# Sparse-attention layer on one core: compression MLP with high and low keys side by side, position term apart, x and key/value weights in one row

## The chip, the cores and the metric

One core of a Trainium2 chip runs the whole program. The metric is the device time of one execution in microseconds; the number compared is the median over runs. A core has the engines PE (TensorE: matmuls and their weight loads), DVE (VectorE), ACT (ScalarE), POOL (GpSimd) and SP (SyncE, which here issues nearly all DMAs). Each engine works through its instructions in order and waits for others by semaphores.

## The reference

One decoder layer of native sparse attention: 256 positions, width 2048, 16 query heads of 128 in 4 groups, one key and one value head per group and branch, all in float32. What matters here is the compressed branch; its keys and values come of a small MLP over blocks of 32 positions, one every 16:

```python
def nsa_compress(kv, pe, w1, w2):
    n_cmp = (kv.shape[1] - CMP_LEN) // CMP_STRIDE + 1          # 15 blocks
    idx = np.arange(n_cmp)[:, None] * CMP_STRIDE + np.arange(CMP_LEN)[None, :]
    blocks = kv[:, idx] + pe[None, None, :, None, :]
    hid = jax.nn.silu(jnp.einsum('bnlgd,lde->bnge', blocks, w1))
    return jnp.einsum('bnge,ef->bngf', hid, w2)

h = x @ w_in            # queries, three pairs of keys and values, gates, z
k_cmp, v_cmp = nsa_compress(kc, pe_k, w1_k, w2_k), nsa_compress(vc, pe_v, w1_v, w2_v)
...                     # compressed, selected and window attention, gated sum
y = (o * silu(z)) @ w_out
x = layer_norm(ALPHA * x + y)
```

## The kernel before

Every float32 operand is split into a rounded high part, written by ACT, and the remainder as low part, written by DVE (`split_into`, L72 to L74). A product is then three fast matmuls: high by high, high by low, low by high. For the projections x stands with high and low part side by side, so that one matmul of 512 columns (L110) does two of the three and one of 256 columns (L113) the third; `join` (L119) adds the halves.

*The key/value pass* (`kv_pass`, L161) comes first: 16 chunks of 128 rows of x and of the 1024 weight columns that give kc and vc, into 8 PSUM banks, 16 matmuls per chunk. x is loaded by `load_x` (L85) into tiles `kt` (4 buffers) and the weights into tiles `big` (8 buffers); chunk 0's weights come as three pieces, one of them on ACT's queue, the rest on SP's. From chunk 13 on the value half is held back (`LATE`) and done at the end. Six matmuls on zeros run ahead of it (`WARM`). The small tables are loaded at chunk 15 (`load_small`).

*Then* `kv_out` joins and splits kc into tiles with columns for 4 groups x 16 blocks and 2 for the position embedding (66 in all, `CM`), two projections of group 0 run (`proj_t`, 1 MB of weights each, loaded into `wraw`, 3 buffers, split in two halves into `whi` and `wlo`, 4 buffers each), `kv_out` does vc, and `compress_hidden` runs the first layer of the MLP for k, for v a little later: 16 rows, three matmuls of 256 columns each (L219 to L221), with the weights `w1` loaded as 1 MB twice and split into halves of 4 rows. PE's order up to the MLP for k is that of the source; the rest is ordered by a planner that gives each engine the ready instruction that comes first in the source. `compress_act` (L226) adds up the partial sums by two float32 matmuls against a 0/1 table `csel`, which also adds the position columns to each block; `compress_out` (L243) is the second layer.

*Then*, per group, `group_proj` (keys, four query heads, bias, a value projection), `attention` for the first 128 positions, `z_proj` (four gate projections) and `attention` for the rest; at the end the output projection, residual and normalization. `compress_act` and `compress_out` stand inside `group_proj(0)`, between key and query projections. Scores of the compressed branch read the columns 256 to 272 of the key tiles, which L323 copies.

## Time and profile before

| | us |
|---|---|
| median of 3 runs (487.21 to 487.33) | 487.32 |
| the profiled execution, its own time | 486.98 |
| its span, first to last instruction | 485.2 |
| PE busy (2822 matmuls) | 475.4 |
| DVE busy | 332.4 |
| ACT busy | 274.4 |
| DMA: 91.41 MB, share of 16 engines' time on SP's queue | 51.4% |

Read the table with care: a busy share is an average over stages, and PE's matmuls overlap, so that its busy time is longer than the sum of their steps. What a step costs on PE is read from the distance between the starts of two instructions in the timeline. The granted clock of PE was 0.997 over the execution.

### The profile page before, as it was taken

How to read it: one execution, taken by the hardware profiler on the slowest of the kernel's cores; microseconds unless marked ns; L12 is line 12 of the kernel's file. 1: busy time of each engine (PE TensorE's matmuls, PEld its weight loads, DVE VectorE, ACT ScalarE, POOL GpSimd, SP SyncE). 2: the span in 40 equal slices, each digit the busy share in tenths (PEclk: the TensorE clock that was granted, in tenths of full speed). 3: DMA queues.
4: the chain of work that ended last, by engine and by line, in shares of the span. 5: the costliest groups of instructions: out<-in, count | busy, mean ns of one | idle time of the engine just before them, and what ended most of it. 6: DMA issues, size and time to landing. Idle time of an engine off the chain costs nothing.

```text
span 485.2 us, 7570 instructions
## 1 busy us (share of the span) xinstructions
PE 475.4 (98%) x2822; PEld 416.8 (86%) x2823; DVE 332.4 (69%) x760; ACT 274.4 (57%) x543; POOL 9.6 (2%) x16
## 2 busy tenths in 40 slices
PE   7999999999999999999999999999999999999994
PEld 4888889899888889888889988888988888888893
DVE  4754887656878656777865686775577775597745
ACT  5653785447665645767555566654476644565411
POOL 1000000000000000000000000000000000000014
PEclk9999999999999999999999999999999999999998
DMA  7992579545443634363644534354436955357204
GB/s 271 404 365 112 174 257 331 202 175 175 173 175 130 225 131 174 99 247 104 224 162 174 173 151 133 153 182 173 151 111 223 377 199 192 140 174 261 86 1 173
DMA packets 18959, 91.41 MB, mean 188 GB/s; under 512 B 2404, under 2 KB 5591, under 8 KB 10219
## 3 DMA queue, kind: packets, MB, share of 16 engines
q1 hardware_dynamic: 18635, 90.54, 51.4%
q8 instruction: 22, 0.36, 0.3%
q10 hardware_dynamic: 288, 0.39, 0.2%
q14 instruction: 14, 0.11, 0.1%
HBM read 88.80 MB, written 2.12 MB: 187 GB/s over the span
## 4 chain that ended last, share of the span: by engine, by line
PE 96%; DMA 1%; DVE 1%; SPq 0%; ACT 0%; issue 0%; DVEq 0%
PE proj L110 33%; PE proj L113 17%; PE proj L509 3%; PE proj L508 3%; PE proj L507 3%; PE proj L337 3%; PE proj L336 3%; PE proj L335 3%; PE tr L430 2%; PE sc L509 2%; PE sc L507 2%; PE sc L508 2%; PE sc L110 1%; PE tr L110 1%; PE sc L383 1%; PE sc L385 1%
## 5 line engine op out<-in xcount | busy, mean ns | idle before, releaser
L110 PE MATMUL proj<-xs,whi 128*128 128x512 f32 x688 | 241.6, 397 | 2.2 <-ACT whi L73 1.8
L74 DVE TENSOR_TENSOR wlo<-wraw,whi 128x1024 fp32r<-128x1024 f32 (+1 forms) x134 | 164.0, 1228 | 89.9 <-ACT whi L73 89.5
L73 ACT ACTIVATE whi<-wraw 128x1024 fp32r<-128x1024 f32 (+1 forms) x134 | 142.1, 1063 | 114.8 <-PE proj L110 51.1
L113 PE MATMUL proj<-xs,wlo 128*128 128x256 f32 x688 | 188.0, 282 | 0.1
L110 PEld LDWEIGHTS proj<-xs,whi 128*128 128x128 f32 x688 | 127.9, 188 | 29.0 <-ACT whi L73 3.3
L113 PEld LDWEIGHTS proj<-xs,wlo 128*128 128x128 f32 x688 | 128.3, 188 | 3.2 <-DVE wlo L74 0.5
L393 ACT ACTIVATE t<-t,m 128x128 f32<-128x128 f32 (+3 forms) x96 | 37.6, 395 | 8.9 <-DVE m L391 8.8
L337 PE MATMUL proj<-wlo,xs 128*128 128x268 f32 x128 | 36.6, 286 | 0.0
L336 PE MATMUL proj<-whi,xs 128*128 128x268 f32 x128 | 36.6, 286 | 0.0
L335 PE MATMUL proj<-whi,xs 128*128 128x268 f32 x128 | 36.4, 285 | 0.0
L74 DVE TENSOR_TENSOR wlo<-big,whi 128x1024 fp32r<-128x1024 f32 (+2 forms) x18 | 19.8, 1106 | 13.7 <-ACT whi L73 11.8
L509 PE MATMUL proj<-whi,big 128*128 128x512 f32 (+1 forms) x76 | 28.6, 377 | 0.0
L508 PE MATMUL proj<-wlo,big 128*128 128x512 f32 (+1 forms) x76 | 28.6, 376 | 0.0
L507 PE MATMUL proj<-whi,big 128*128 128x512 f32 (+1 forms) x76 | 27.7, 376 | 0.0
L73 ACT ACTIVATE whi<-big 128x1024 fp32r<-128x1024 f32 (+2 forms) x18 | 17.3, 965 | 16.8 <-PE tr L110 9.1
L335 PEld LDWEIGHTS proj<-whi,xs 128*128 128x128 f32 x128 | 24.0, 188 | 0.4
L336 PEld LDWEIGHTS proj<-whi,xs 128*128 128x128 f32 x128 | 24.1, 188 | 0.1
L337 PEld LDWEIGHTS proj<-wlo,xs 128*128 128x128 f32 x128 | 24.1, 188 | 0.0
L122 DVE SCALAR_TENSOR_TENSOR join<-proj,join 128x256 f32<-128x256 f32 x43 | 17.9, 419 | 7.9 <-ACT join L121 7.9
L433 ACT ACTIVATE ph<-tr 128x512 fp32r<-128x512 f32 x24 | 14.1, 598 | 15.7 <-PE tr L430 15.6
L434 DVE TENSOR_TENSOR pl<-tr,ph 128x512 fp32r<-128x512 f32 x24 | 16.2, 687 | 5.9 <-ACT ph L433 5.5
L393 ACT ACTIVATION_READ_ACCUMULATOR t<-t,m 128x1 f32 x96 | 18.2, 190 | 0.0
(182 smaller groups left out, 662.2 us busy)
## 6 DMA issues: line engine op xcount, KB each, us to landing
wraw<-in_wt SPq DMA_DIRECT2D x40, 1024.0 KB, 4.9
wraw<-in_wo SPq DMA_DIRECT2D x16, 1024.0 KB, 5.0
wraw<-in_wv SPq DMA_DIRECT2D x8, 1072.0 KB, 5.5
...
wraw<-in_w_k SPq DMA_DIRECT2D x2, 1024.0 KB, 5.2
wraw<-in_w_v SPq DMA_DIRECT2D x2, 1024.0 KB
...
```

Of the source, the lines that this page charges most:

```text
L73: act.activation(hi, src, AF.Copy)
L74: pin(dve.tensor_tensor(lo, src, hi.bitcast(F32), op=ALU.subtract))
L110: pe.matmul(acc, hi, xk(k), start=(k == 0), stop=False)
L113: pe.matmul(acc[:, :SEQ], lo, xh(k), start=False, stop=(k == KC - 1))
L122: dve.scalar_tensor_tensor(t, acc[:, :SEQ], scale, t, op0=ALU.mult, op1=ALU.add)
L335: pe.matmul(a, xh(k)[:, ts], hi[:, k4, :], start=(k == 0), stop=False)
L336: pe.matmul(a, xl(k)[:, ts], hi[:, k4, :], start=False, stop=False)
L337: pe.matmul(a, xh(k)[:, ts], lo[:, k4, :], start=False, stop=(k == KC - 1))
L393: act.activation(tt, tt, AF.Exp, bias=m[:, i:i + 1], scale=-1.0, accum_out=den[:, i:i + 1])
L507: pin(pe.matmul(y, ah, hi[:, h2, c0:c1], start=(hq == 0 and h == 0), stop=False))
L508: pin(pe.matmul(y, ah, lo[:, h2, c0:c1], start=False, stop=False))
L509: pin(pe.matmul(y, al, hi[:, h2, c0:c1], start=False, stop=(hq == 3 and h == 3)))
```

## The change

x and the key/value weights are laid out as one array of 16 chunks, 128 rows of 1280 floats (5 KB): one load per chunk into the `wraw` tiles, chunk 0 in two pieces on SP's queue. x is split chunk by chunk (before: mostly by two), the weights of chunk 1 in two halves. Warm-up matmuls are 8 for 6. The small tables are loaded at chunk 8, in source order on SP's queue, with the one-hot table and 1 MB of w1 behind them. The key tiles hold high and low part side by side: the first layer is one matmul with all 128 weight columns against the high part of w1 and one with the 64 high ones against the low part. The position embedding leaves the key tiles; `add_pos` sums pe[l] * w1[l] over the 32 rows l on DVE into a 128x128 tile, for which w1 is loaded a second time in four pieces of 1 MB into the tile `t1` (1 buffer), and a third matmul in `compress_act` adds its column sums to each valid block. `compress_act` for k moves behind the query heads of group 0, that for v, `compress_out` and the copies of L323 behind the value projection. The host-side layout follows.

```diff
--- before.py
+++ after.py
@@ -32,11 +32,12 @@
 VW = 2 * P + 3 * HPG
 LU = 384
 KTW = 4 * P + 16
-CM = NG * 16 + 2
-FIRST = ((0, 256), (256, 512), (512, 1024))
-CUTS_X = (0, 1, 2, 4, 6, 8, 10, 12, 14, 16)
+CM = NG * 16
+FIRST = ((0, 512), (512, 1280))
+SPLITS = {0: ((0, 256), (256, 512), (512, 1024)), 1: ((0, 512), (512, 1024))}
 LATE = 13
-WARM = 6
+SMALL_AT = 8
+WARM = 8
 WARM_END = 8
 PARTS = ((0, 320), (320, 512))
 
@@ -82,16 +83,13 @@
 
     X2 = [None] * 4
 
-    def load_x(k0, k1):
-        raw = sb.tile([P, KTW], F32, name="kt", bufs=4)[:, :(k1 - k0) * SEQ]
-        raw = raw.rearrange("p (k s) -> p k s", s=SEQ)
-        nc.sync.dma_start(raw, A["xT"][k0 // 2][:, k0 % 2:k0 % 2 + k1 - k0, :])
-        c, o = divmod(k0, 4)
+    def split_x(k, raw):
+        c, o = divmod(k, 4)
         if o == 0:
             X2[c] = [xp.tile([P, 2, 2 * SEQ], F32R, name="xs") for _ in range(2)]
-        t = X2[c][o // 2][:, o % 2:o % 2 + k1 - k0, :]
-        hi, lo = t[:, :, :SEQ], t[:, :, SEQ:]
-        if k0 == 0:
+        t = X2[c][o // 2][:, o % 2, :]
+        hi, lo = t[:, :SEQ], t[:, SEQ:]
+        if k == 0:
             dve.tensor_copy(hi, raw)
             dve.tensor_tensor(lo, raw, hi.bitcast(F32), op=ALU.subtract)
         else:
@@ -137,9 +135,11 @@
         for n, shape in (("peT_k", [P, CLEN]), ("peT_v", [P, CLEN]), ("w2_k", [P, P]), ("w2_v", [P, P]),
                          ("rel", [2 * CSTRIDE, NH]), ("gmask", [P, 3 * HPG]), ("signs", [5, 2])):
             t = const.tile(shape, F32, name=n)
-            nc.sync.dma_start(t, A[n])
+            keep(nc.sync.dma_start(t, A[n]))
             small[n] = t
-        nc.sync.dma_start(csel, A["csel"])
+        keep(nc.sync.dma_start(csel, A["csel"]))
+        keep(nc.sync.dma_start(onehot, A["onehot"]))
+        keep(nc.sync.dma_start(first_w1, A["w1_k"][:, :8, :]))
 
     ident = const.tile([P, P], F32, name="ident")
     make_identity(nc, ident)
@@ -160,20 +160,14 @@
 
     def kv_pass():
         for k in range(KC):
-            if k in CUTS_X:
-                load_x(k, CUTS_X[CUTS_X.index(k) + 1])
-            raw = sb.tile([P, CSTRIDE * CM], F32, name="big", bufs=8)[:, :1024].rearrange("p (k n) -> p k n", k=1)
-            src = A["wkvc"][k][:, None, :]
-            if k == 0:
-                hi, lo = (wp.tile([P, 1, 1024], F32R, name=n, bufs=4) for n in ("whi", "wlo"))
-                for i, (n0, n1) in enumerate(FIRST):
-                    (act if i == 0 else nc.sync).dma_start(raw[:, :, n0:n1], src[:, :, n0:n1])
-                for n0, n1 in FIRST:
-                    split_into(hi[:, :, n0:n1], lo[:, :, n0:n1], raw[:, :, n0:n1], keep)
-            else:
-                nc.sync.dma_start(raw, src)
-                hi, lo = split_w(raw, 0, 1)
-            if k == KC - 1:
+            raw = wp.tile([P, SEQ + 1024], F32, name="wraw", bufs=3)
+            for n0, n1 in FIRST if k == 0 else ((0, SEQ + 1024),):
+                nc.sync.dma_start(raw[:, n0:n1], A["xw"][k, :, n0:n1])
+            split_x(k, raw[:, :SEQ])
+            hi, lo = (wp.tile([P, 1, 1024], F32R, name=n, bufs=4) for n in ("whi", "wlo"))
+            for n0, n1 in SPLITS.get(k, ((0, 1024),)):
+                split_into(hi[:, 0, n0:n1], lo[:, 0, n0:n1], raw[:, SEQ + n0:SEQ + n1], keep if k == 0 else lambda i: i)
+            if k == SMALL_AT:
                 load_small()
             kv_mms(k, hi, lo, 0, NG)
             if k < LATE:
@@ -184,16 +178,18 @@
             kv_mms(*args, NG, 2 * NG)
 
     def kv_out(which, name):
-        hi, lo = (sb.tile([P, CSTRIDE, CM], F32R, name="big", bufs=8) for _ in range(2))
+        kvc[name] = sb.tile([P, CSTRIDE, 2 * CM], F32R, name="big", bufs=4)
         for g in range(NG):
-            view = [t[:, :, g * 16:(g + 1) * 16].rearrange("p l n -> p n l") for t in (hi, lo)]
+            view = [kvc[name][:, :, c + g * 16:c + (g + 1) * 16].rearrange("p l n -> p n l") for c in (0, CM)]
             split_into(*view, join(accs[NG * which + g]).rearrange("p (n l) -> p n l", l=CSTRIDE))
-        view = [t[:, :, 64:66].rearrange("p l a -> p a l") for t in (hi, lo)]
-        split_into(*view, small["peT_" + name].rearrange("p (a l) -> p a l", a=2))
-        kvc[name] = hi, lo
-
-
-    csel = sb.tile([P, SEQ], F32, name="zth", bufs=1)[:CM].rearrange("p (a n) -> p a n", a=2)
+
+
+    onehot = sb.tile([P, 512], F32, name="ph", bufs=2)[:33, :LU]
+    first_w1 = sb.tile([P, 8, 2 * P], F32, name="t1", bufs=1)
+    csel = sb.tile([P, SEQ], F32, name="zth", bufs=1)[:, :2 * CM].rearrange("p (a n) -> p a n", a=2)
+    valid = const.tile([P, CM], F32, name="valid")
+    pool.memset(valid, 1.0)
+    pool.memset(valid.rearrange("p (g n) -> p g n", g=NG)[:, :, NCMP:], 0.0)
     kc_hi = const.tile([P, NG, 16], F32R, name="kc_hi")
     kc_lo = const.tile([P, NG, 16], F32R, name="kc_lo")
     vcs = const.tile([P, NG, P], F32R, name="vcs")
@@ -207,26 +203,48 @@
     phc = const.tile([P, HPG, P], F32R, name="phc")
     pool.memset(phc.bitcast(F32), 0.0)
 
+
+    pos = {n: const.tile([P, P], F32, name="pos_" + n) for n in "kv"}
+
+    def add_pos(name):
+        for l0 in (0, 8):
+            raw = first_w1 if (name, l0) == ("k", 0) else sb.tile([P, 8, 2 * P], F32, name="t1", bufs=1)
+            if raw is not first_w1:
+                nc.sync.dma_start(raw, A["w1_" + name][:, l0:l0 + 8, :])
+            for l in range(8):
+                for a in range(2):
+                    w, o = raw[:, l, a * P:(a + 1) * P], 16 * a + l0 + l
+                    pe_l = small["peT_" + name][:, o:o + 1]
+                    if o == 0:
+                        dve.tensor_scalar(pos[name], w, pe_l, None, op0=ALU.mult)
+                    else:
+                        dve.scalar_tensor_tensor(pos[name], w, pe_l, pos[name], op0=ALU.mult, op1=ALU.add)
+
+
     def compress_hidden(name):
-        part = bank("proj")[:CM, :2 * P]
-        hi, lo = kvc[name]
+        part = bank("proj")[:, :2 * P]
+        hl = kvc[name]
         for i in range(2):
             raw = load_w(A["w1_" + name][:, 8 * i:8 * i + 8, :], 8, 2 * P)
             for j in range(2):
                 wh, wl = split_w(raw, 4 * j, 4 * j + 4)
                 for l4 in range(4):
                     l = 8 * i + 4 * j + l4
-                    pe.matmul(part, hi[:, l, :], wh[:, l4, :], start=(l == 0), stop=False)
-                    pe.matmul(part, hi[:, l, :], wl[:, l4, :], start=False, stop=False)
-                    pe.matmul(part, lo[:, l, :], wh[:, l4, :], start=False, stop=(l == CSTRIDE - 1))
-        ps_sb = sb.tile([P, 512], F32, name="pl", bufs=2)[:CM, :2 * P]
+                    last = l == CSTRIDE - 1
+                    for lo in (True, False) if last else (False, True):
+                        if lo:
+                            pe.matmul(part[:CM], hl[:, l, :CM], wl[:, l4, :], start=False, stop=False)
+                        else:
+                            pe.matmul(part, hl[:, l, :], wh[:, l4, :], start=(l == 0), stop=last)
+        ps_sb = sb.tile([P, 512], F32, name="pl", bufs=2)[:, :2 * P]
         act.activation(ps_sb, part, AF.Copy)
         return ps_sb
 
     def compress_act(name, ps_sb):
-        acc = bank("sc")[:, :P]
+        acc = bank("sc")[:, :CM]
         for i in range(2):
-            pe.matmul(acc, ps_sb[:, i * P:(i + 1) * P], csel[:, i, :], start=(i == 0), stop=(i == 1))
+            pe.matmul(acc, ps_sb[:, i * P:(i + 1) * P], csel[:, i, :], start=(i == 0), stop=False)
+        pe.matmul(acc, pos[name], valid, start=False, stop=True)
         th = sb.tile([P, 512], F32, name="a", bufs=1)[:, :64]
         act.activation(th, acc[:, :64], AF.Tanh, scale=0.5)
         src = acc[:, :64].rearrange("p (g n) -> p g n", g=NG)
@@ -274,8 +292,6 @@
 
 
     rel_aug = const.tile([33, NH], F32, name="rel_aug")
-    onehot = sb.tile([P, 512], F32, name="ph", bufs=2)[:33, :LU]
-    nc.sync.dma_start(onehot, A["onehot"])
     dve.memset(rel_aug[32:33, :], MASKED)
     dve.tensor_scalar(rel_aug[0:32, :], small["rel"], -1.0, None, op0=ALU.mult)
     pu = bank("o")
@@ -306,7 +322,6 @@
             split_into(kt[0][:, o:o + P], kt[1][:, o:o + P], acc[:, half * P:(half + 1) * P])
         if g == 0:
             hv = compress_hidden("v")
-            compress_act("k", hk)
         split_into(kt[0][:, 272:528], kt[1][:, 272:528], join(early[1] if g == 0 else proj_t(10 * g + 1)))
         st["kt"] = kt
         st["q"] = []
@@ -315,12 +330,11 @@
             qt = [sb.tile([P, SEQ], F32R, name="q", bufs=10) for _ in range(2)]
             split_into(qt[0], qt[1], acc)
             st["q"].append(qt)
-            if g == 0 and h == 0:
-                compress_act("v", hv)
             if g == 0 and h == 1:
-                compress_out()
-        for t, s in zip(kt, (kc_hi, kc_lo)):
-            dve.tensor_copy(t[:, 256:272], s[:, g, :].bitcast(F32))
+                add_pos("k")
+        if g == 0:
+            compress_act("k", hk)
+            add_pos("v")
         st["bias"] = load_bias(g)
         accs = [bank("proj") for _ in range(2)]
         for h in range(2):
@@ -340,6 +354,11 @@
         for t in range(2):
             split_into(v[0][:, t, :], v[1][:, t, :], accs[t][:, :2 * P])
             act.activation(gt[:, t, :], accs[t][:, 2 * P:VW], AF.Tanh, scale=0.5)
+        if g == 0:
+            compress_act("v", hv)
+            compress_out()
+        for t, s in zip(kt, (kc_hi, kc_lo)):
+            dve.tensor_copy(t[:, 256:272], s[:, g, :].bitcast(F32))
         st["v"], st["gt"] = v, gt
         return st
 
@@ -441,8 +460,8 @@
 
     def gate(g, qt, o_ps):
         if qt == 0:
-            AH[g] = sb.tile([P, HPG, SEQ], F32R, name="big", bufs=8)
-            AL[g] = sb.tile([P, HPG, SEQ], F32R, name="big", bufs=8)
+            both = sb.tile([P, 2, HPG, SEQ], F32R, name="big", bufs=4)
+            AH[g], AL[g] = both[:, 0], both[:, 1]
         qs = slice(qt * P, (qt + 1) * P)
         a = sb.tile([P, HPG, P], F32, name="a", bufs=1)
         for h in range(HPG):
@@ -666,8 +685,7 @@
         return a.reshape(-1, P, a.shape[-1]).transpose(1, 0, 2)
 
     arr = {"x": x}
-    arr["xT"] = np.stack([rows(x.T[k:k + 2 * P]) for k in range(0, DM, 2 * P)])
-    arr["wkvc"] = w[:, 2048:3072].reshape(KC, P, 1024)
+    arr["xw"] = np.concatenate([x.T.reshape(KC, P, SEQ), w[:, 2048:3072].reshape(KC, P, 1024)], axis=2)
     wt = []
     for g in range(NG):
         cols = [3072 + g * P, 4096 + g * P]
@@ -699,11 +717,12 @@
     oh[:, :127] = 0.0
     oh[32, :127] = 1.0
     arr["onehot"] = oh
-    cs = np.zeros((CM, 2, P), np.float32)
+    cs = np.zeros((2, CM, 2, CM), np.float32)
     for g in range(NG):
         for n in range(NCMP):
             j = 16 * g + n
-            cs[j, 0, j] = cs[64, 0, j] = cs[j + 1, 1, j] = cs[65, 1, j] = 1.0
+            cs[:, j, 0, j] = cs[:, j + 1, 1, j] = 1.0
+    cs = cs.reshape(2 * CM, 2, CM)
     arr["csel"] = cs
     gm = np.ones((P, HPG, 3), np.float32)
     gm[:31, :, 0] = 0.0
```

## Rows read from the trace of the kernel before

**Rows 1.** page, engine table: busy us, share of the span, instructions

```profile
PE 475.4 (98%) x2822; PEld 416.8 (86%) x2823; DVE 332.4 (69%) x760; ACT 274.4 (57%) x543; POOL 9.6 (2%) x16
```

**Rows 2.** PE timeline, start: start us, length, line, tiles, count

```profile
1.19 2.74 PE L131 MATMUL tr<-zero 128*128 128x512 bf16 x6 [1.19 <-DVE zero L127]
...
4.31 1.19 PE L110 MATMUL proj<-xs,whi 128*128 128x512 f32 x3 [0.38 <-DVE xs L96]
...
9.49 0.96 PE L110 MATMUL proj<-xs,whi 128*128 128x512 f32 x3 [1.79 <-ACT whi L73]
...
12.73 0.85 PE L110 MATMUL proj<-xs,whi 128*128 128x512 f32 x3
...
15.55 0.86 PE L110 MATMUL proj<-xs,whi 128*128 128x512 f32 x3
...
51.92 0.40 PE L110 MATMUL proj<-xs,whi 128*128 128x512 f32 x1
```

**Rows 3.** windows: us, busy us and instructions by engine, clock, DMA share, GB/s

```profile
5.00:6.00 1.00, 1.00 (x8) 0.87 (x6) 0.00 (x0) 0.63 (x1) 0.00 (x0) 1.00 0.36 116
...
7.70:9.50 1.80, 0.01 (x2) 0.01 (x1) 0.33 (x2) 1.11 (x2) 0.00 (x0) 1.00 1.02 412
...
20.00:50.00 30.00, 30.00 (x172) 26.22 (x171) 15.43 (x19) 13.47 (x18) 0.00 (x0) 1.00 0.64 247
...
63.00:73.00 10.00, 10.00 (x80) 8.99 (x79) 9.17 (x15) 9.43 (x17) 0.00 (x0) 1.00 0.71 262
...
63.00:111.00 48.00, 48.00 (x337) 44.11 (x336) 33.09 (x51) 27.96 (x43) 0.53 (x1) 1.00 0.66 243
```

**Rows 4.** timeline of ACT, chunk 1's high-part split

```profile
8.38 1.06 ACT L73 ACTIVATE whi<-big 128x1024 fp32r<-128x1024 f32 x1 [0.84 <-DMA big<-in_wkvc]
```

**Rows 5.** DMA issues by line: count, KB each, median us to landing

```profile
wraw<-in_wt SPq DMA_DIRECT2D x40, 1024.0 KB, 4.9
```

**Rows 6.** timeline of SP's queue: the slowest of the small loads to issue

```profile
22.06 1.33 SPq L140 DMA_DIRECT2D gmask<-in_gmask  x1
```

**Rows 7.** timeline of PE, end of the pass and first MLP rows

```profile
50.05 0.40 PE L113 MATMUL sc<-xs,wlo 128*128 128x256 f32 x2
...
50.29 0.40 PE L113 MATMUL tr<-xs,wlo 128*128 128x256 f32 x2
...
63.15 0.28 PE L219 MATMUL proj<-whi,big 128*66 128x256 f32 x1
...
67.37 0.28 PE L219 MATMUL proj<-whi,big 128*66 128x256 f32 x1
```

**Rows 8.** chain of work that ended last: bias matmul, then combining k's sums

```profile
67.65 0.74 PE o L282 x2
...
72.87 0.45 PE sc L229 x4
```

**Rows 9.** timelines of DVE and PE, compression MLP

```profile
64.33 1.23 DVE L74 TENSOR_TENSOR wlo<-wraw,whi 128x1024 fp32r<-128x1024 f32 x1 [0.68 <-ACT whi L73]
...
71.62 1.23 DVE L74 TENSOR_TENSOR wlo<-wraw,whi 128x1024 fp32r<-128x1024 f32 x1
...
74.80 0.28 PE L220 MATMUL proj<-wlo,big 128*66 128x256 f32 x1
```

**Rows 10.** groups by shape: busy us, mean ns, idle before

```profile
L449 DVE SCALAR_TENSOR_TENSOR a<-o,zs 128x128 f32<-128x128 f32 x32 | 7.4, 283 | 1.1 <-PE o L439 0.6
```

**Rows 11.** timeline of DVE, dependent and independent small instructions

```profile
120.68 0.23 DVE L396 RECIPROCAL den<-den 128x12 f32<-128x12 f32 x1
...
120.94 0.17 DVE L399 TENSOR_TENSOR coef<-coef,den 128x12 f32<-128x12 f32 x1
...
141.37 0.69 DVE L449 SCALAR_TENSOR_TENSOR a<-o,zs 128x128 f32<-128x128 f32 x3
```

**Rows 12.** timelines of DVE and PE, first V projection tile of group 0

```profile
92.72 1.28 DVE L74 TENSOR_TENSOR wlo<-wraw,whi 128x1072 fp32r<-128x1072 f32 x1
...
100.09 0.29 PE L337 MATMUL proj<-wlo,xs 128*128 128x268 f32 x1
```

## The prediction

> **What bounds the kernel now.** I read the table of engines first: TensorE (PE) is busy 475.4 us, 98% of the span of 485.2 [rows 1]. A busy PE is not yet a PE without waits, so I read next where it waited. The order of its instructions at the start shows all of it: after six warm-up matmuls the first real one starts at 4.31 us, chunk 0 is done at about 7.7, chunk 1 starts at 9.49, chunk 2 at 12.73, chunk 3 at 15.55 (a full-speed chunk is thus 2.82 us), and the first projection after the key/value pass at 51.92 [rows 2]. Sixteen chunks at 2.82 us from 4.31 would end at 49.4, so 2.5 us are lost, nearly all in 7.70 to 9.50, where PE did nothing [rows 3]. From 12.7 us to about 475 us PE has no gap, so there each PE microsecond removed is worth a microsecond, but only while VectorE and ScalarE (ACT), which split every weight tile into a high and a low part ahead of PE, keep ahead of it. The windows by stage say where they hardly do: in 63 to 73 us (the compression MLP) VectorE (DVE) is busy 9.17 of 10 us [rows 3].
>
> The sum is made against the profiled execution: 486.98 us, that is 485.2 of span and 1.8 around it. The median of the runs shown, 487.32, is 0.34 above it; I take the savings off the median.
>
> **Part 1, the 5 KB rows (forecast: 1.3 us gained).** Before, chunk 0 comes as four loads (1 and 2 KB rows) on two queues, x and w apart; after, as two loads on SP, 262 and 393 KB, then one 655 KB load per chunk. In chunk 0 little is gained: the warm-up grows from 6 to 8 matmuls, at 2.74 us for 6 [rows 2] that is 1.19 + 8 x 0.457 = 4.85 for the first real matmul in place of 4.31; 4.85 + 2.82 = 7.67 is the old end of chunk 0, since the old chunk 0 had inner waits. What can go is the wait for chunk 1. DMA moved only 116 GB/s in 5 to 6 us but 412 GB/s in 7.7 to 9.5 [rows 3]. If this dip came of the small loads, chunk 1 lands in time and the pass runs 7.67 + 15 x 2.82 = 50.0, 1.9 us earlier than 51.92. If the dip stays, chunk 1's w lands about as late as now (ACT started on it at 8.38 and took 1.06 us [rows 4]), but it is split in two halves, so PE starts after half a split, some 0.3 us sooner, and chunk 1 itself (3.24 us against 2.82) loses 0.4 less: 0.7. No row tells the two apart; I take the middle, 1.3.
>
> Against it stand two costs inside the pass. The chunks now use 3 buffers where there were 8 (w) and 4 (x), so chunk k+3 is issued only when chunk k is split. A 1 MB load lands in 4.9 us [rows 5]; for 655 KB I estimate 4 us (between 0.64 of it and all of it), which with some 3 us of splitting makes 7 us for 3 chunks against 3 x 2.82 = 8.5 on PE: it holds with 1.5 us to spare per round. The small loads move from chunk 15 to chunk 8 and gain the one-hot table and 1 MB of w1. All are issued on SP, where the mask alone takes 1.33 us [rows 6]; with a quarter to a third of that for each of the nine others I estimate 4.5 us in all; chunk 9's load and the first projection weights stand behind them. The lead that the 1.5 us per round have built by chunk 8 (about 4 us) covers this; without the cover it costs what is missing, 0 to 1.3 us. I cost it at nothing and give its failure to a rival.
>
> **Part 2, two matmuls per row (3.76 us off PE).** The MLP issues 3 x 16 x 2 = 96 matmuls of 256 columns with 66 weight columns, 36 of them from 63.15 to 67.37, 0.117 us each [rows 7]. After it, 64: one with 128 weight columns (high and low keys side by side), one with 64. The wider weight load costs nothing: low-part matmuls with 128 weight columns and 256 columns already follow each other at 0.24 us for two in the pass from 50.05 to 50.29 [rows 7]. 32 x 0.1175 = 3.76 us go.
>
> **Part 3, what comes back on PE (-0.4 us).** Combining the partial sums takes, for k and v each, two 4-byte matmuls, run as 4 passes of 128 columns in 0.45 us [rows 8]; it becomes six passes of 64 columns. Bounds: six at half the price, 0.34, a gain of 0.1 each; six at the full price, 0.67, a loss of 0.2. The weight load of each pass stays whole for 64 columns, and the row is nearest to a full price, so I take 0.2 lost, 0.4 for both.
>
> **Part 4, splits that no longer keep up (-1.5 us).** PE now eats half a w1 load (one split tile) in 8 x 0.1175 = 0.94 us, before 1.41; DVE needs 1.23 for its low part. Only 4 split tiles exist, so the lead is small: the fourth tile of w1 k is done at 65.56 and the fourth of w1 v at 72.85, its low part first used at 74.80 [rows 9]. In the new order PE would want that last tile at 63.15 + 4 x 0.94 + 0.74 (the bias matmul in between [rows 8]) + 3 x 0.94 = 70.5. If DVE keeps its order, PE waits 2.4 us; if the key joins and splits for v (some 2.1 us of DVE between these two tiles) find another place, 0.3. The next weights tell a like story: their buffer is free when the tile ending at 65.56 is split, then 4.9 us of load and 2.3 of splitting, 72.8, for a PE that comes at 71.4. These overlap, not add. I take 1.5; the ends are 0.3 and 2.4.
>
> **Part 5, the position term on DVE (0 us in the forecast).** The position rows leave the splits (four small pieces, off the path) and come back as 64 DVE instructions on 128x128 floats, 32 for k and 32 for v, each adding to the result of the one before. An instruction of this kind and size lasts 283 ns [rows 10]. Independent ones follow at about 0.2 us (three in 0.69), but where one needs the last one's result, the next starts some 0.03 us after its end (120.68 + 0.23, next at 120.94) [rows 11]. So 64 x 0.21 = 13.4 us at the least and 64 x 0.32 = 20.5 at the most; the chain is dependent, I take 20.5. The Trainium skill (VectorE: DVE Perf Modes, Terms, "DRAIN") says that the next instruction can't issue until the pipe of the last is empty, dependent or not; that would make 64 x 0.283 = 18.1 us, and the rival on DVE below would then just not come about. The overlapped starts of the independent ones don't agree with it.
>
> What hides it: DVE is idle 14.6 us in 20 to 50 us and 14.9 us in 63 to 111 us [rows 3]. The first 1 MB of w1 k is loaded for this during the pass, so its 16 instructions (5 us) fit in the first stretch; the other 48 (15.4 us) stand against 14.9 less the 1.9 us by which that stage shrinks, plus the lead of the splits. The step that needs the result moved back too: the k half behind the four query heads, the v half and the copies of compressed keys behind the V projection, so attention of group 0 (first scores just after 111 us) waits for them. PE has the four gate projections of group 0 to run meanwhile. The three later 1 MB loads share one buffer: each is issued on SP when the 16 instructions before it are done, and the weight loads behind it on SP wait too. The wider stride of the keys' split tile (512 for 264 bytes) I cost at nothing, since PE runs a projection over these splits; without that cover a slower write would add to part 4.
>
> **Sum:** 1.3 + 3.76 - 0.4 - 1.5 = 3.16 us; 487.32 - 3.16 = 484.2. By its own ends: gains of 0.7 + 3.76 - 0.4 - 2.4 = 1.7 to 1.9 + 3.76 - 0.2 - 0.3 = 5.2 us, with the last terms' better ends.
>
> **Rivals.**
> - *All of it is had* (482.1): the dip goes and DVE finds room, 5.2 us. For it: DMA reaches 412 GB/s as soon as 4 KB rows are all that is queued [rows 3]. Against: DVE at 9.17 of 10 us.
> - *One gain does not come.* Either the pass gains nothing, because 3 buffers and the small loads at chunk 8 hand back the 1.3 (485.5); or the MLP does on PE what it says but the splits set its pace entirely, and the 1.86 of parts 2 to 4 goes (486.0). I write 485.7. For it: chunks and small loads share SP's order. Against: the spare 1.5 us per round.
> - *DVE becomes the bound, slower* (488.5). One mechanism: the position instructions stand in DVE's order in front of low-part splits, in 63 to 111 us, and one of their w1 loads is not there when they come up, so DVE is held for up to 4.9 us [rows 5] with splits behind it, and PE waits for those. Price: if all 64 fall in there, 20.5 + 4.9 = 25.4 us against 13.0 of idle DVE and the leads that the splits have, 2.0 us at 72.85 [rows 9] and 6.1 in the V projection (split by 94.00, used at 100.09 [rows 12]): 25.4 - 13.0 - 8.1 = 4.3 lost, 1.2 more than gained. It decides from 13.0 + 8.1 + 3.2 = 24.3 us of position work and waiting in that stretch. With 16 instructions done during the pass it is 15.4 + 4.9 = 20.3, below it.
>
> **How the numbers follow.** Forecast 0.46, all of it 0.15, one gain missing 0.23, DVE the bound 0.16. The time is the forecast's, 484.2. Within 0.2% (1 us, about what a measurement of this kernel can tell from no change) lies a part of the third and the milder fourth: 0.11; slower 0.13; faster 0.76. The range reaches from below the best case, 481.8, to 487.9, which leaves out the worst of the slower case.
>
> **What would show it.** PE: chunk 1 starting near 7.7 (part 1; at 9 the dip stayed); the first projection after the pass near 50.6; 64 MLP matmuls at 0.1175; gaps of 1 to 2 us between the MLP and the first query head, put down to DVE or ACT splits; then no gap up to the end. DVE: 64 position instructions at 0.3 us, 16 of them before 50 us. It would be wrong if PE waits for low parts later than 75 us, or if a chunk after 8 waits for its load.

## The result, and the profile after

The changed kernel is slower: 490.35 us (median of 7) against 487.33 for the kernel before on the same chip, ratio 1.0075 [1.0059, 1.0091]. Its profiled execution took 490.07 us, of which 488.3 is span. A profile shows one execution, which can lie 1 to 3 us from the median of its kernel. Forecast were 484.2 us and a range up to 487.9.

Table of engines of the changed kernel (busy us, share of the span, instructions), to hold beside [rows 1]: PE does as much as before, DVE has 19.3 us more.

```profile
PE 474.9 (97%) x2796; PEld 415.3 (85%) x2797; DVE 351.7 (72%) x830; ACT 274.2 (56%) x549; POOL 9.7 (2%) x18
```

Timeline of PE, beside [rows 2]: the starts of chunks 1, 8, 9, 10 and 11, the first projection behind the pass, two gaps in the MLP stage. In brackets stand the idle time ahead and who ended it.

```profile
9.43 0.94 PE L108 MATMUL proj<-xs,whi 128*128 128x512 f32 x3 [1.21 <-ACT whi L74]
...
29.06 0.85 PE L108 MATMUL proj<-xs,whi 128*128 128x512 f32 x3
...
34.64 0.97 PE L108 MATMUL proj<-xs,whi 128*128 128x512 f32 x3 [2.60 <-ACT whi L74]
...
39.23 1.26 PE L108 MATMUL proj<-xs,whi 128*128 128x512 f32 x3
...
42.42 0.86 PE L108 MATMUL proj<-xs,whi 128*128 128x512 f32 x3
...
56.40 0.39 PE L108 MATMUL proj<-xs,whi 128*128 128x512 f32 x1
...
73.48 0.66 PE L246 MATMUL sc<-zth,pl 128*128 128x64 f32 x4 [1.05 <-ACT pl L240]
...
74.65 0.35 PE L238 MATMUL proj<-whi,big 128*128 128x256 f32 x1 [0.52 <-DVE big L75]
```

Chunk 1 is at 9.43 (9.49 before). Chunks then follow at 2.8 us up to chunk 8. Chunk 9 starts 5.58 us behind chunk 8, of which 2.60 is a wait, and takes 4.59 us itself; chunk 10 takes 3.19. Against 2.8 us per chunk these three steps lose 4.9 us. The first projection starts at 56.40, 4.48 us later than in [rows 2], since some 0.4 us had been gained at the first chunks. From there to the warm-up ahead of the last stage the changed kernel is 1.57 us quicker (478.50 - 56.40 = 422.10 us against 475.59 - 51.92 = 423.67). So the pass lost 4.5 us and the rest gained 1.6, where the prediction had 1.3 and 1.86 gained.

Windows of the changed kernel, columns as in [rows 3]:

```profile
30.00:40.00 10.00, 7.12 (x31) 5.72 (x30) 8.07 (x18) 4.43 (x8) 0.00 (x0) 0.83 0.82 320
...
60.00:70.00 10.00, 10.00 (x63) 8.72 (x62) 10.00 (x19) 7.52 (x13) 0.00 (x0) 1.00 0.67 225
...
70.00:80.00 10.00, 8.44 (x62) 7.41 (x61) 10.00 (x16) 8.76 (x18) 0.53 (x1) 1.00 0.84 293
```

Behind the wait for chunk 9 the granted clock is 0.83 in the mean of 10 us (part of them at 1.2 GHz in place of 2.4): this, and 0.28 us of wait for a low part, makes chunk 9 take 4.59 us. In 60 to 80 us DVE is busy all the time (in the kernel before 9.17 of 10 from 63 to 73 [rows 3]).

What held chunk 9: SP's queue and the load, for which ACT waits; DVE is held at the same time. From the page the time from issue to landing of a chunk's load, then SP, ACT and DVE:

```profile
wraw<-in_xw SPq DMA_DIRECT2D x15, 640.0 KB, 5.2
```

```profile
16.97 3.40 SPq L165 DMA_DIRECT2D wraw<-in_xw  x2
...
20.43 0.43 SPq L138 DMA_DIRECT2D peT_k<-in_peT_k  x1
...
26.51 0.33 SPq L142 DMA_DIRECT2D t<-in_w_k  x1
...
26.94 1.75 SPq L165 DMA_DIRECT2D wraw<-in_xw  x3
```

```profile
26.03 1.04 ACT L74 ACTIVATE whi<-wraw 128x1024 fp32r<-128x1024 f32 x1
...
33.22 0.42 ACT L74 ACTIVATE xs<-wraw 128x256 fp32r<-128x256 f32 x1 [6.15 <-DMA wraw<-in_xw]
```

```profile
31.72 0.29 DVE L219 TENSOR_SCALAR pos_k<-t,peT_k 128x128 f32<-128x128 f32 x1 [3.39 <-DMA t<-in_w_k]
...
32.04 1.90 DVE L221 SCALAR_TENSOR_TENSOR pos_k<-t,peT_k,pos_k 128x128 f32<-128x128 f32 x5
...
33.86 0.42 DVE L75 TENSOR_TENSOR xs<-wraw,xs 128x256 fp32r<-128x256 f32 x1
```

The load of chunk 8 is the second of the two issued from 16.97. Nine small loads and 1 MB of w1 follow in order up to 26.84, and only then chunk 9 (26.94), whose buffer (chunk 6) had been split by 22.1. Its load lands at 33.22, and ACT waits 6.15 us for it: this is PE's wait of 2.60. DVE meanwhile stands at the first position instruction, which waits 3.39 us for its w1; five more of them (1.90 us) are ahead of chunk 9's low part. Most of that lies inside the wait for the load and costs PE only the 0.28 us for the low part. The lead that the pass had is read at chunk 8: its high part is done at 27.07 and PE comes to it at 29.06, 2.0 us later.

### The profile page after: what moved, and what is told of

Same layout as the page of the kernel before. It is cut to its first block, busy times and chain, and to the rows that moved or that the text cites. A ratio compares the mean times of both kernels' runs of the same rounds, so it can differ in the third digit from the quotient of the medians.

```text
span 488.3 us, 7604 instructions
## 1 busy us (share of the span) xinstructions
PE 474.9 (97%) x2796; PEld 415.3 (85%) x2797; DVE 351.7 (72%) x830; ACT 274.2 (56%) x549; POOL 9.7 (2%) x18
## 4 chain that ended last, share of the span: by engine, by line
PE 90%; DMA 5%; DVE 3%; issue 1%; ACT 1%; SPq 0%; DVEq 0%
PE proj L108 31%; PE proj L111 16%; DMA wraw<-in_xw 4%; PE proj L526 3%; PE proj L528 3%; PE proj L527 3%; PE proj L351 3%; PE proj L350 3%; PE proj L349 3%; PE tr L449 2%; PE sc L526 2%; PE sc L528 2%; PE sc L527 2%; PE sc L402 1%; PE sc L403 1%; PE sc L404 1%
## 5 line engine op out<-in xcount | busy, mean ns | idle before, releaser
L75 DVE TENSOR_TENSOR wlo<-wraw,whi 128x1024 fp32r<-128x1024 f32 (+3 forms) x153 | 183.9, 1205 | 79.6 <-ACT whi L74 79.0
L74 ACT ACTIVATE whi<-wraw 128x1024 fp32r<-128x1024 f32 (+3 forms) x153 | 159.0, 1044 | 110.6 <-PE proj L108 43.2
L119 ACT ACTIVATE join<-proj 128x256 f32<-128x256 f32 x43 | 15.7, 369 | 5.2 <-DVE pos_v L221 4.0
L74 ACT ACTIVATE xs<-wraw 128x256 fp32r<-128x256 f32 x15 | 6.3, 418 | 21.5 <-DMA wraw<-in_xw 21.3
```

The source lines that it names most:

```text
L74: act.activation(hi, src, AF.Copy)
L75: pin(dve.tensor_tensor(lo, src, hi.bitcast(F32), op=ALU.subtract))
```

## The experiments

All ratios are to the kernel before, timed on the same chip. Four ideas were set against each other: the order of loads on SP (A), position instructions that hold DVE (B), the key MLP's combining matmul moved into the value MLP (C), and the values' split that comes too late for a shorter MLP (D). Rivals E, F and G are told where they come up. The letters of the recorded expectations are these from e9 on; in e1 to e4 and in e8 Theory B is another one, that three buffers are too few, and in e5 to e7 Theory D is what is B here. That three buffers alone make the gap falls with e1 and e8, which have three and no gap like it in the pass.

**Small loads elsewhere (e1 to e4).** e1: all ten behind the last chunk.

```
-SMALL_AT = 8
+SMALL_AT = KC - 1
```

> The ten small and first-w1 loads stand behind the last chunk's load (chunk 15) instead of behind chunk 8's. Theory A (the order on SP's queue holds chunk 9's load back): PE's gap after chunk 8 goes, the pass ends near 51.5 us instead of 56.4, the time is about 485.5; a gap of up to 1 us can come at the first projection, whose weights now stand behind the ten. Theory B (three buffers are too few for 5 KB rows whatever stands between): PE still waits for a chunk of the pass for 2 us or more, 488 to 490.

Measured: 1.0152 [1.0116, 1.0188]. e2: one small load behind each of chunks 3 to 11, the first w1 behind the last chunk.

```
+            if k != 3 + j:
+                continue
...
+        if k == KC - 1:
+            keep(nc.sync.dma_start(first_w1, A["w1_k"][:, :8, :]))
```

> The same loads in the same order, but one small load behind each of the chunks 3 to 11 and the first 1 MB of w1 behind chunk 15. Theory A: no gap in the pass after chunk 2 and none at its end, the pass ends near 51.5, the time is about 485.3. Theory B: a gap of 2 us or more stays, 488 to 490.

Measured: 1.0133 [1.0101, 1.0165]. e3: only the 1 MB of w1 taken out of the ten.

```
-        keep(nc.sync.dma_start(first_w1, A["w1_k"][:, :8, :]))
...
-            if raw is not first_w1:
+            if True:
```

> Only the 1 MB of w1 is taken out of the ten loads behind chunk 8; the nine small ones stay there. If the time that SP needs to issue the loads is the cause, chunk 9's load is issued only 0.4 us sooner, the gap stays above 2 us and the time near 490. If the 1 MB in front of it on the DMA engines is the cause, chunk 9 lands 2.6 us sooner, the gap after chunk 8 all but goes, PE's clock doesn't fall, and the time is near 485.5 to 486.5. Theory B: no change, 490.

Measured: 1.0091 [1.0063, 1.0119]. e4: four buffers for the chunks.

```
-            raw = wp.tile([P, SEQ + 1024], F32, name="wraw", bufs=3)
+            raw = sb.tile([P, 2 * CSTRIDE * CM], F32, name="big", bufs=4)[:, :SEQ + 1024]
```

> The chunks are loaded into four buffers (those that later hold the keys) instead of three; the ten loads stay behind chunk 8. Theory B: the gap goes, 485.5. Theory A: the ten loads are issued earlier, at about 17 to 23 us, but chunk 9's still stands behind them; the gap shrinks from 2.8 us to 0 to 1.5, 486 to 487.5, and the start of chunk 1 stays at 9.4 us.

Measured: 1.0119 [1.0095, 1.0142]; its gap stands at chunk 4 (3.86 us). There the planner put 3 MB of later weights on SP's queue ahead of chunk 4's load, so e4 does not test the fourth buffer. The gap at chunk 9 is gone in e1, e2 and e3, and e3 says which load makes it: without the 1 MB of w1 the other nine, still ahead of chunk 9, leave no gap there. Chunk 9's load is issued at 26.38 in e3 and lands at 30.34, 0.56 and 2.88 us sooner than in the change (the w1 load, no longer pinned, was issued at 2.58 us there). e5 below has the nine loads behind chunk 8, no w1, and no gap either. But none of the four is faster for it. Timelines of PE, of e1, e2 and e3:

```profile
54.23 0.75 PE L108 MATMUL proj<-xs,whi 128*128 128x512 f32 x1 [2.88 <-DVE join L120]
...
74.37 0.76 PE L246 MATMUL sc<-zth,pl 128*128 128x64 f32 x4 [2.45 <-ACT pl L240]
...
76.36 0.55 PE L238 MATMUL proj<-whi,big 128*128 128x256 f32 x1 [1.24 <-DVE big L75]
```

```profile
49.84 1.01 PE L111 MATMUL proj<-xs,wlo 128*128 128x256 f32 x3 [2.37 <-DVE wlo L75]
...
73.22 0.66 PE L250 MATMUL sc<-zth,pl 128*128 128x64 f32 x4 [1.18 <-ACT pl L244]
...
78.22 0.55 PE L242 MATMUL proj<-whi,big 128*128 128x256 f32 x1 [4.35 <-DVE big L75]
```

```profile
71.75 1.12 PE L245 MATMUL sc<-zth,pl 128*128 128x64 f32 x4 [2.04 <-ACT pl L239]
```

and of DVE in e2:

```profile
47.98 0.29 DVE L223 TENSOR_SCALAR pos_k<-t,peT_k 128x128 f32<-128x128 f32 x1 [3.83 <-DMA t<-in_w_k]
```

In e1 PE waits 6.6 us behind the pass, for a DVE join, for ACT's copy of the key sums and for a split. In e2 DVE stood 3.83 us at the first position instruction, waiting for w1, with the split of the last chunk behind it; PE then waited 2.37 us for that split and 5.5 us in the MLPs (this execution took 496.33 us, the median is 494.04). e3 loses 0.80 us at 47.31, for a position instruction, 2.04 and 0.53 in the MLPs, and its clock is 0.66 from 70 to 80 us. Idea A alone falls: the pass's gap is real, but the time comes back at the next place where DVE is short.

**Without the position term (e5, e6).** Both leave the position term out of what is computed; e5 has the small loads of the change, e6 those of e2.

```
-        pe.matmul(acc, pos[name], valid, start=False, stop=True)
...
-                add_pos("k")
...
-            add_pos("v")
```

> The changed kernel without the position term: no DVE sum over the rows, no second load of w1, no third matmul when the partial sums are combined; the nine small loads stay behind chunk 8. Theory D (the position instructions in DVE's order, and their waits for the second copy of w1, hold back the splits that PE needs): DVE is never held by a load of w1, PE's gaps in the compression MLP shrink below 1 us in all, and the time is 484 to 485, some 7 us below the run with the first w1 load taken out of the ten. Theory A (the small loads on SP are the main cost): a gap in the pass stays and the time is 488 or more.

Measured: 0.9982 [0.9969, 0.9995].

> Without the position term as before, and the small loads one behind each of the chunks 3 to 11. Theory D: 10 us below the same order with the position term (494.0), at 483.5 to 484.5: the pass 0.5 us shorter than before, 3 us gained in the MLP. If the MLP on PE is bound by the splits anyway, 486.

Measured: 0.9991 [0.9971, 1.0012]. So the position term with its loads costs 0.0093 (4.5 us, uncertain by 1.0) as the change places it, and the two matmuls per row, with the new pass, give 0.4 to 0.9 us without it, not 3.8. By the profiles the 4.5 us lie in the pass: the first projection starts at 51.12 in e5, 5.28 us sooner than in the change, and from there to the last stage's warm-up e5 takes 423.71, no less than the kernel before and 1.61 more than the change. PE in e5 says where the 3.8 us stay:

```profile
68.53 0.66 PE L244 MATMUL sc<-zth,pl 128*128 128x64 f32 x4 [1.33 <-ACT pl L238]
...
69.75 0.36 PE L236 MATMUL proj<-whi,big 128*128 128x256 f32 x1 [0.57 <-DVE big L75]
```

```profile
70.00:80.00 10.00, 10.00 (x60) 9.38 (x59) 7.92 (x11) 6.13 (x10) 0.00 (x0) 0.83 0.96 331
```

1.33 us for ACT's copy of the key sums, 0.57 for a split of the values, and then 10 us at a mean clock of 0.83, where it stays at 1.00 in the change.

**The pass alone (e8):** the kernel before with the new loads (and e2's small loads), its own MLP.

```
+            raw = wp.tile([P, SEQ + 1024], F32, name="wraw", bufs=3)
+            for n0, n1 in FIRST if k == 0 else ((0, SEQ + 1024),):
+                nc.sync.dma_start(raw[:, n0:n1], A["xw"][k, :, n0:n1])
```

> The kernel before with only the key/value pass changed: 5 KB rows into three buffers, eight warm-up matmuls, the small loads one behind each of the chunks 3 to 10; the MLP and the position columns are those of before. Chunk 1 starts at 9.4 us as in the changed kernel, chunk 2 at 12.3: the pass ends 0.4 us sooner than before and the time is 486.5 to 487.5. Theory B (three buffers are too few): 488 or more.

Measured: 0.9998 [0.9984, 1.0011]. Chunk 1 starts at 9.11, no other wait follows: the rows of 5 KB are worth nothing that can be measured, and cost nothing.

**The position sum elsewhere (e7, e11).** e7 makes it on POOL:

```
+                pool.tensor_tensor(w, w, pe_l, op=ALU.mult)
+            for n in (4, 2, 1):
+                pool.tensor_tensor(raw[:, :n, :], raw[:, :n, :], raw[:, n:2 * n, :], op=ALU.add)
```

> The small loads one behind each of the chunks 3 to 11, and the position term summed on POOL instead of DVE: per 1 MB of w1 two multiplications of 128x1024 by the embedding and a tree of additions in place, some 10 us on POOL, 40 in all. Theory D: nothing that PE needs stands behind a wait for w1, so the time is that of the run without the position term plus 0 to 1 us, 484 to 485.5. If it is the 4 MB of extra loads and not DVE's order, 488 to 492 as with the sum on DVE.

Measured: 1.0216 [1.019, 1.0242], a clear miss. DVE and POOL in e7:

```profile
51.62 2.32 DVE L75 TENSOR_TENSOR wlo<-wraw,whi 128x1024 fp32r<-128x1024 f32 x1
...
60.79 1.21 DVE L75 TENSOR_TENSOR wlo<-wraw,whi 128x1024 fp32r<-128x1024 f32 x1
...
67.12 2.78 DVE L75 TENSOR_TENSOR big<-join,big 128x256 fp32r<-128x256 f32 x1
...
69.81 0.41 DVE L120 SCALAR_TENSOR_TENSOR join<-tr,join 128x256 f32<-128x256 f32 x1
```

```profile
47.91 6.62 POOL L223 TENSOR_TENSOR t<-t 128x1024 f32<-128x1024 f32 x3
...
66.19 6.52 POOL L223 TENSOR_TENSOR t<-t 128x1024 f32<-128x1024 f32 x3
```

While POOL adds, a DVE split of 1024 columns takes 2.32 us in place of 1.21 (at 60.79, between POOL's stretches), one of the values 2.78 in place of 0.65 (at 58.18); the join, which reads one operand from PSUM, stays at 0.41. The Trainium skill (SBUF — State Buffer, SBUF: two separate sides) says that a DVE instruction with two SBUF inputs and a GpSimd instruction that reads SBUF lock one pair of ports against each other for their whole length. These rows agree.

e11 reads the w1 tiles that the MLP loads anyway, so that no second load exists:

```
+                for l4 in range(4):
+                    pos_term(name, 8 * i + 4 * j + l4, raw[:, 4 * j + l4, :])
```

> The whole computation: small loads spread as in e2, and the position instructions read the w1 tiles that the MLP itself loads, so that there is no second load of w1 and no wait for one; they then lie in the MLP stage, where the planner may put them. Theory B by its first half (the wait for a missing w1 load): no position instruction waits for a DMA ahead of a split, 0.999 to 1.003 of the kernel before (e6 is 0.9991). By its second half (their work among the splits of a stage in which DVE is 8.6 to 9.8 of 10 us busy): 20 us of work into 20 us of that stage, TensorE waits of 4 to 8 us there, 1.008 to 1.016 as in e2.

Measured: 1.0315 [1.0291, 1.034], worse than either case: waits from 55 to 91 us, the longest 2.91 at 81.78 for a high-part split whose w1 had not landed, clock 0.50 in 70 to 80. The position instructions hold the weight buffers longer, and the next loads start late (DMA share 0.41 and 0.34 in 50 to 70 us). Since it takes away the second load and delays the first, the run tells neither what that load costs nor what DVE's work costs by itself.

**Where the MLP's gain is (e9, e12, e14, e16).** The first three leave the position term out. e9 is e6 with the combining matmuls pinned at their place in the source:

```
+            keep(pe.matmul(acc, ps_sb[:, i * P:(i + 1) * P], csel[:, i, :], start=(i == 0), stop=(i == 1)))
```

> The small loads are spread over the pass and the position term is left out, as in e6 (0.9991 of the kernel before), and the key MLP's combine matmul (line 244) is now pinned behind the query heads, where it stands in the source, instead of being moved into the value MLP. In e6 TensorE waited 1.33 us at that matmul for ACT's pl, then 0.56 us for a split of the values, and its granted clock was 0.83 in the 10 us that followed. Theory C (the two matmuls per row save their 3.8 us, but the moved combine matmul opens the gap and the clock falls behind it): without the first wait the second has no reason either, some 1.9 us come back and 1.0 to 1.7 us of clock with them, 0.992 to 0.995 of the kernel before, no wait over 0.3 us in the value MLP. Rival D (the value MLP is bound by the splits of DVE and ACT): the wait of 1.3 us moves to the next matmul that needs a split, the clock still falls, 0.998 to 1.000.

Measured: 0.9999 [0.9983, 1.0015]. Idea C falls, D stands. Timelines of PE and DVE, and the windows behind the gap (PE busy, clock, DMA share, GB/s):

```profile
70.35 0.55 PE L239 MATMUL proj<-whi,big 128*128 128x256 f32 x1 [2.97 <-DVE big L75]
```

```profile
66.17 3.50 DVE L75 TENSOR_TENSOR wlo<-wraw,whi 128x1024 fp32r<-128x1024 f32 x3
...
69.57 0.63 DVE L75 TENSOR_TENSOR big<-join,big 128x256 fp32r<-128x256 f32 x1
```

```profile
70.30:75.00 4.70, 4.65 (x22) 0.50 0.91 354
...
75.00:80.00 5.00, 5.00 (x32) 0.94 0.97 283
```

The first matmul of the value MLP waits 2.97 us for the last split of the values, which stands behind three weight splits (3.50 us) on a DVE without idle time from 60 to 70 us. For 4.7 us behind it the clock is 0.50, that is 1.2 GHz: the value MLP takes 6.2 us (70.35 to 76.57), where 32 matmuls at full clock take 3.76. The wait and the clock together, 5.4 us, are more than the change took off PE. (This execution took 488.28 us; the median is 487.25.)

e12 puts the value MLP behind the first query head, e14 the key MLP behind head 0 and the value MLP behind head 1 (shown is e14):

```
-            hv = compress_hidden("v")
...
+            if g == 0 and h == 0:
+                hk = compress_hidden("k")
+            if g == 0 and h == 1:
+                hv = compress_hidden("v")
```

> As e9 (position term left out, small loads spread, combine matmuls in place; 0.9999 of the kernel before), with the value MLP moved behind the first query head, so that 5.6 us of TensorE's work stand between the two MLPs. In e9 TensorE waited 2.97 us at the value MLP's first matmul for DVE's last split of the value keys (DVE 10.00 busy of 10 us there), and the granted clock was 0.72 in the 10 us behind it. Theory D (the shorter MLP makes the values' split due 4 us earlier than the full DVE can deliver, and the clock falls behind the gap): no wait over 0.3 us, no clock under 0.95 after 10 us, so 3.0 us and some 2 to 2.8 us of clock come back: 0.989 to 0.994. Rival F (the splits of the stage as a whole bound it): a wait of 1 to 3 us turns up at the first query head or in the value MLP, 0.996 to 1.000.

Measured: 0.9959 [0.9945, 0.9974]; one wait is left behind chunk 1, 1.34 us for the bank behind the key MLP, and a clock of 0.86 behind it. The result lies between the bands written for D and for F, with the sign of F.

> As e12 (position term left out; 0.9959 of the kernel before) with the key MLP behind query head 0 and the value MLP behind head 1, so that three projections stand between the pass and the first MLP instead of two. In e12 the first head waited 1.34 us for the bank that the key MLP's result leaves, ACT's copy pl standing behind late splits, and the granted clock was 0.86 in the following 10 us. Theory D carried on (all that the MLP saves comes free where the splits have time): no wait over 0.3 us between the pass and the scores, clock 0.97 or more, so 1.3 us and 1.0 to 1.4 us of clock more than e12: 0.990 to 0.993. Rival F (the splits of the stage as a whole bound it): a wait of 1 to 2 us at another matmul of the stage, 0.995 to 0.998.

Measured: 0.99 [0.9883, 0.9918], no wait between chunk 0 and the last group. This is the band written for D, and F falls. Two of its windows:

```profile
60.00:70.00 10.00, 10.00 (x59) 8.19 (x58) 8.01 (x14) 7.36 (x16) 0.00 (x0) 1.00 0.71 233
...
70.00:80.00 10.00, 9.89 (x68) 8.89 (x67) 8.11 (x10) 7.18 (x11) 0.00 (x0) 1.00 1.01 375
```

e16 makes the same move in the kernel before.

> The kernel before with one edit: its key MLP behind query head 0 and its value MLP behind head 1 (with what follows them one head later). Theory D (before waits for no split there, so the move gives nothing by itself, and e14's 4.9 us are the two matmuls per row with the gap taken away): 0.998 to 1.002. Rival G (the order alone is what helps, and two matmuls or three make no odds): 0.990 to 0.994.

Measured: 1.0004 [0.9993, 1.0015]. Rival G falls: the move by itself is worth nothing. e14 against e16, the same order with two matmuls per row and with three, is 0.0104, 5.1 us with an uncertainty of 1.0 (two chips). It holds, beside the matmuls, the new pass (nothing in e8, though chunk 1 starts 0.8 us sooner in e14's profile than in [rows 2]) and the position columns that e14 leaves out. By the profiles e14 is 3.16 us quicker than the kernel before from the first projection to the last warm-up (420.51 against 423.67). So the two matmuls per row come out near their 3.8 us, but only where the splits have time.

**The whole computation again (e10, e13, e15, e18, e17).** The position term is back on DVE, its 64 instructions pinned one by one where DVE has room; w1 comes in quarters of 512 KB, the later ones from POOL's queue. Of e18, the steps in the pass, at the query heads and at the value tiles:

```
+            pos_step({8: 2, 9: 2, 10: 2, 11: 2, 12: 2, 13: 2, 14: 2}.get(k, 0))
...
+                pos_step((2, 4, 14, 14)[h])
...
+                pos_step((8, 8)[t])
```

e10 stands on e9:

> The whole computation, position term on DVE: e9 with the 64 position instructions pinned where DVE was least busy in e6: 2 behind each chunk from 8 to 15, 8 behind query heads 0 and 1, 12 behind heads 2 and 3, 4 behind each value tile, none between the pass and the first head. Their w1 tiles come in eight quarters of 512 KB through two buffers, the first two from the SP queue behind chunks 5 and 6, the rest from the POOL queue, so that no wait for a buffer holds SP. Theory B (the position term costs time because its instructions stand in DVE's order where a w1 load is missing, or between the splits of the MLP stage): pinned like this it costs under 1 us over e9, 0.993 to 0.998. Rival E (the 20 us of DVE work cost what they cost wherever they stand before the scores): 4 to 5 us over e9, 1.002 to 1.006 with waits for splits at the query heads.

Measured: 1.0053 [1.0032, 1.0075]; 1.49 us lost at chunk 15, beside the third quarter's load, and 2.55 at the value MLP. e13 stands on e12:

> The whole computation: e12 with the position term on DVE, its 64 instructions pinned: 2 behind each chunk from 7 to 13, then 2, 10, 14 and 14 behind the query heads and 5 behind each value tile, with the third quarter of w1 loaded from the SP queue behind the last chunk and the later ones from the POOL queue. In e10 (1.0053) a chunk waited 1.49 us beside the third quarter's load and the value MLP 2.55 us. Theory B with D (the instructions cost by the place where they stand): within 1 us of e12, 0.990 to 0.996, the version that beats both. Rival E (20 us of DVE work before the scores cost 3 to 5 us wherever they stand): 0.997 to 1.003, with waits for splits at heads 1 to 3 or the value tiles.

Measured: 1.0019 [1.0001, 1.0037]. e15 stands on e14:

> The whole computation: e14 with the position term on DVE, pinned: 2 instructions behind each chunk from 5 to 11, then 0, 4, 14 and 14 behind the query heads and 9 behind each value tile; the first two quarters of w1 from the SP queue behind chunks 3 and 4, the later ones from the POOL queue. In e13 (1.0019) TensorE waited 0.4 us at chunk 8, 0.97 us at the end of the pass, 1.73 us for the bank behind the key MLP. Theory B with D (the place decides): within 1.5 us of e14, 0.991 to 0.996, faster than both kernels. Rival E (the 20 us of DVE work cost 3 us or more wherever they stand before the scores): 0.997 to 1.002.

Measured: 0.9958 [0.9941, 0.9975]. This computes all and beats both kernels. e18 is e15 with the loads later:

> The whole computation: e15 (0.9958) with the first two quarters of w1 loaded behind chunks 6 and 7 instead of 3 and 4, two position instructions behind each chunk from 8 to 14, and the last one of each of these two quarters behind query head 0, so that no later quarter is loaded during the pass; then 4, 14 and 14 instructions behind heads 1 to 3 and 8 behind each value tile. In e15 chunk 1 began at 9.81 (8.71 in e14), chunk 5 waited 0.43 us and the first projections 0.25 us, together about 2 of the 3.4 us between the two profiles. Theory B (the loads' place costs, not the DVE work): no wait in the pass behind chunk 1, 0.991 to 0.995. Rival E (the DVE work costs what it did): 0.995 to 0.998.

Measured: 0.9974 [0.9961, 0.9987]. PE in e15 and in e18:

```profile
21.66 0.97 PE L108 MATMUL proj<-xs,whi 128*128 128x512 f32 x3 [0.43 <-ACT whi L74]
```

```profile
72.74 0.39 PE L111 MATMUL proj<-xs,wlo 128*128 128x256 f32 x1 [0.37 <-DVE wlo L75]
...
82.60 0.50 PE L108 MATMUL proj<-xs,whi 128*128 128x512 f32 x1 [0.46 <-ACT whi L74]
...
83.86 0.39 PE L111 MATMUL proj<-xs,wlo 128*128 128x256 f32 x1 [0.76 <-DVE wlo L75]
```

Over its own twin without the term, the pinned term costs 0.0054 (e10), 0.0060 (e13), 0.0058 (e15) and 0.0074 (e18): 2.6 to 3.6 us, each uncertain by 1.1 to 1.3, in other places each time (by the profiles, e15 loses 1.7 us in the pass behind chunk 1 and 0.6 behind the pass, e18 2.0 behind the pass, 1.6 of them in waits). e10, e13 and e18 lie in the bands written for E; e15's ratio lies in that for B, but its distance from e14 is E's. So some 3 us were lost wherever I put the term, against 4.5 (uncertain by 1.0) as the change places it, which is not clear of noise. Clear of it is only the worst place: e2 against its twin e6 is 0.0142, 6.9 us (two chips). Whether the 3 us are DVE's work or its 4 MB of loads stays open: only e11 has the work without a second load, and it holds other loads back.

e17 is the change itself with the move of e14 and nothing else:

> The changed kernel with the same single edit: key MLP behind head 0, value MLP behind head 1; ten small loads behind chunk 8 and the position instructions where the planner puts them, as in the change. It was 1.0075. Theories A, B and D together (4.5 us of it are the held chunk 9 in the pass, which the move doesn't touch; 1.6 us and more are the MLP stage): the gap of 2 to 3 us at chunk 9 stays, the waits in the MLPs go, 1.000 to 1.005. Rival (the loss moves on to another place, as it did in e1 to e4): 1.006 to 1.012.

Measured: 1.0047 [1.0023, 1.0071]. The ratio lies in the range written for A, B and D together, the path only in part: the gap at chunk 9 stays (1.59 us), but so does a wait in the MLP stage. This profile is of an execution of 492.64 us, near the upper end of 485.94 to 492.86 with a median of 489.58, so that wait need not be in the others. PE and DVE there:

```profile
76.54 0.36 PE L238 MATMUL proj<-whi,big 128*128 128x256 f32 x1 [2.54 <-DVE join L120]
```

```profile
73.73 0.35 DVE L221 SCALAR_TENSOR_TENSOR pos_k<-t,peT_k,pos_k 128x128 f32<-128x128 f32 x1
...
74.54 0.37 DVE L221 SCALAR_TENSOR_TENSOR pos_k<-t,peT_k,pos_k 128x128 f32<-128x128 f32 x1
...
75.98 0.75 DVE L120 SCALAR_TENSOR_TENSOR join<-proj,join 128x256 f32<-128x256 f32 x2
```

The planner has put a position instruction behind nearly every split of that stage (nine from 63.7 to 74.9 us), and the join that the key MLP's bank waits for comes that much later.

## Why the prediction was wrong

What came is nearest to the first half of the second rival, that 3 buffers and the small loads at chunk 8 "hand back the 1.3"; but they took 4.9 us where that rival had no more than the gain. The third rival's mechanism (position instructions ahead of splits, a w1 load not there), with "slower" as its sign, made only 0.28 us of it in the changed kernel; it made 2.37 in e2 and 0.80 in e3. Its sign came, by another path. By its own steps:

- **What bounds the kernel: right**, and the condition that DVE and ACT "keep ahead of it" was the one that decided.
- **Part 1: the gain was taken too high, the cost at nothing.** The dip stayed (9.43): 0.06 us at chunk 1, 0.46 at chunk 2, against 1.3; e8 measures nothing. Chunk 1's start lies anywhere from 7.56 to 10.06 us in the profiles of kernels with the new loads, so one profile can't tell what load size does to it.
- **The failed step: the two costs inside the pass, 3 buffers and the loads behind chunk 8, put at nothing (0 to 1.3 if uncovered), since a lead of 4 us was to cover them.** They cost 4.9 us: chunk 9's load came late, PE waited 2.60 us for it and then ran at a lower clock. Three terms were mis-sized. A chunk's load lands in 5.2 us (median), not in the 4 estimated, so the spare time per round of three chunks is 8.5 - 8.2 = 0.3 us and not 1.5, and the lead at chunk 8 was 2.0 us, not 4. SP needs 6.4 us for the ten loads (20.43 to 26.84), not 4.5. And the 1 MB of w1 was counted as an issue on SP only, not as 1 MB ahead of chunk 9 on the same queue; without it, in e3, chunk 9's load lands 2.9 us sooner and the gap is gone. The text named the sign to look for, "a chunk after 8 waits for its load", and it came. It also took "from chunk 15 to chunk 8" from the source: in the trace of before the planner issues the small loads one or two at a time from 14.7 to 25.3 us (a mask at 22.06 [rows 6]), and chunk 9's weights, the second of the two below, were on the queue by 12.6 us, with 8 buffers; in the change that chunk's load is issued at 26.94. What was new is that all the small loads stand in one block, pinned, with 1 MB at its end, ahead of a load that is due.

```profile
11.55 1.02 SPq L174 DMA_DIRECT2D big<-in_wkvc  x2
```

- **Part 2: right on PE, not in time.** High and low matmuls follow at 0.12 us (below), and 32 of them are gone. Where the splits have time 3.2 of the 3.76 us show (e14, behind the pass); as the change orders them, e5's and e6's profiles show nothing gained behind the pass, the changed kernel's 1.57.

```profile
67.65 0.28 PE L238 MATMUL proj<-whi,big 128*128 128x256 f32 x1
...
67.77 0.28 PE L236 MATMUL proj<-wlo,big 128*64 128x256 f32 x1
```

- **Part 3: right in sign**, small either way: four passes of 64 columns take 0.66 us in the row at 73.48, no less than the four of 128 in the same view of before (0.61 us at 72.71).
- **Part 4: right in place and mechanism, mis-sized by what follows it.** The waits were 1.57 us here (1.05 of them for ACT's copy of the key sums, which part 4 did not name), 1.9 in e5 and 2.97 in e9, against 1.5 with ends of 0.3 and 2.4. Missing was the price of a gap: TensorE's granted clock was 1.00 in all windows of [rows 3], and no term of the sum asked what it does behind a new wait. It cost 2.5 us in e9 and 1.9 at chunks 9 and 10, and nothing in the changed kernel's MLPs.
- **Part 5: wrong at 0.** The instructions are of the size expected, a little above its upper end: five in a run in 1.90 us, 0.38 each, single ones 0.34, against 0.32. 16 of them ran during the pass, as forecast; 7 ran from 53 to 60 us, nine in 60 to 80, where DVE has next to no idle time, and 32 behind 83. In the changed kernel what cost was the load made for them: the MLP's waits were no longer than without the term (1.57 us against 1.9 in e5). In the other orders the idle time added up over whole stretches (14.6 and 14.9 us) did not hide all of the term: it cost 6.9 us in e2 and 2.6 to 3.6 where I put it.
- **The third rival** had the mechanism and looked in 63 to 111 us only, with 24.3 us of work and waiting as its threshold. In e2 it needed far less: one instruction and one load, in the pass (47.98). In the changed kernel it is not what cost the time.
